# Four of the eight head tiles of the shared keys as seven Strassen block products

## The chip, the cores and the metric

The kernel runs on 1 core of one Trainium2 chip. The metric is the device time in microseconds (us). Before the change, three runs took 1932.31, 1932.89 and 1933.20 us; the median is 1932.89 us. A separate profiled execution took 1931.65 us.

## The reference

One inference step of a two-layer decoder (D_MODEL 1024, 8 heads of 128, 512 prompt rows and 32 sample rows, all float32). Layer 0 has a feed-forward block, a gated token mixer, a second feed-forward block and a gated embedding. From its result one shared set of keys, values and log-forget values is computed, and layer 1 attends to them. The change lies in the keys of that shared projection:

```python
def shared_kv(h, kv_norm, w_kvf, b_f, k_norm):
    bsz, L, _ = h.shape
    xs = rmsnorm(h, kv_norm)
    kvf = xs @ w_kvf
    k = rmsnorm(kvf[..., :D_ATT].reshape(bsz, L, N_HEADS, HEAD_DIM), k_norm)
    v = kvf[..., D_ATT:2 * D_ATT].reshape(bsz, L, N_HEADS, HEAD_DIM)
    logf = jax.nn.log_sigmoid((kvf[..., 2 * D_ATT:] + b_f).astype(jnp.float32))
    return k, v, logf
```

`k`, `v` and `logf` are outputs, and the attention of layer 1 reads them back.

## The kernel before

**Layout.** Activations lie transposed: 8 chunks of 128 features by T = 544 columns (512 prompt, 32 sample). A matmul has a 128x128 stationary weight block and streams 272 columns (HT), half of the 544. Float32 precision comes from pairs: each operand is split into a rounded high part and a remainder, `hi` and `lo`, and a product is three matmuls, hi·hi, hi·lo and lo·hi (`mm`, L286, L290, L292). A head tile of the keys (`k_tile`) is one output of 128 features: 8 weight blocks, 3 products, 2 halves, so 48 matmuls of 272 columns, accumulated in one `ps` tile (two PSUM banks; three such tiles exist). A group of values (`v_group`, L892 to L894) is 96 matmuls of 256 columns in one `ps` tile, and then 16 small ones for the sample rows (L903).

**The weight stream.** All weights pass through one list, `pieces`, in the order of use. `_load` (L209) brings 512 KB by a DMA on SP's queue; `_split` makes `hi` by a CAST on ACT (L242) and `lo` by a subtraction on DVE (L243). `unit()` hands out the next piece and prepares those ahead (2 pieces split, 2 sums, 4 loads ahead). The feed-forward blocks already use Strassen's scheme: `seven` forms, from four quarter blocks of a weight, seven pieces, four of which are sums on DVE (`_sum`, L228); `forms` makes the matching sums of the activations (L352 on ACT, L356, L358, L359 on DVE, and two splits, L330 on ACT with L331 on DVE).

**The stage of the keys and values.** `kv` follows a table, `KV_ORDER`. Each entry between the bars is a step: `k0` is a head tile, `c` the columns step, `v0:` a value group with what stands beside it; after the tile's step come the norms (`s` statistics, `r` fetch a row, `n` norm) and the preparations for the next feed-forward block (`p`, `f`). The statistics of four heads (`stats`, L795 on PE, then `rsqrt_steps`: L386 on ACT, L389, L392, L393 on DVE) go out to memory as `rows` and come back broadcast over 128 partitions (L811), and the norm of a head (L954 on DVE) multiplies by such a row. The very first tiles give the row statistic `rstd` of the residual stream (`tile_rstd`: L403 on ACT, L404 on DVE, L408 on PE, then L386 to L393 again). The columns step (L855, L865) needs it, and every tile's eviction (L845) multiplies by it. The chain of log-forget values (`forget`) runs beside the tiles: L976 on PE, small steps L978 to L994 on DVE, one exponential on ACT (L980, with an ACT table load), then L1001 on PE.

**What sets the order.** Each engine works through its instructions in order and waits at semaphores. In this stage a scheduler sets that order when the program is built; SP's queue holds all the DMAs of the stage.

Of the kernel before, what the change touches and what calls it, by code (L numbers as in the profile page):

```python
# [26 lines left out]
ALU = mybir.AluOpType  # L27
AX = mybir.AxisListType

P = 128  # L30
D = 1024
# [5 lines left out]
T = SEQ + NS  # L37
HT = T // 2
# [14 lines left out]
NKP = NC_ // 2  # L53
# [3 lines left out]
SEVEN = "1562734"  # L57
# [9 lines left out]


KV_ORDER = """
:k0|:k1|c|:k2|:k3|v0:,s0,,r0 r1|:k4 n0 r2|:k5 n1 r3|:k6 n2|:k7 n3|v1:,s1,p0,r4 r5 p1|v2:n4 p2,r6,n5 p3 f0,r7 p4|v3:n6 p5 f1,n7,p6,p7  # L70
""".strip().split("|")


# [1 line left out]
G_KV, G_GV, G_K, G_Q = 64, 72, 80, 81  # L75
# [13 lines left out]
def woven(x):  # L89

    return x.rearrange("p (a b) -> p b a", a=2)


def turns(out):

    return out.rearrange("p (b a) -> p b a", a=2)


def unwoven(out):

    return out.rearrange("p (b a) -> p a b", a=2)


def halves(x):

    return x.rearrange("p (a b) -> p a b", a=2)
# [32 lines left out]
class Builder:  # L139
# [127 lines left out]
    def unit(self):  # L267

        self.prepare()
        return self.take()  # L270
# [76 lines left out]
    def forms(self, h, gcol, n, xs):  # L347

        nc = self.nc
        x = self.big()  # L350
        for a in range(2):
            nc.scalar.activation(x[:, a, :], h[2 * n + a], AF.Copy, scale=self.gain(gcol + 2 * n + a))  # L352
        t13, t24 = self.tmp(), self.tmp()
        two = lambda t: t.rearrange("p (a b) -> p a b", a=2)
        f13, f24 = self.big(F32R), self.big(F32R)
        nc.vector.tensor_tensor(two(t13), x[:, :, HT:], two(x[:, 0, :]), ALU.subtract)  # L356
        self.split_pair(f13, t13)
        nc.vector.tensor_tensor(t24[:, :HT], x[:, 1, HT:], t13[:, :HT], ALU.subtract)  # L358
        nc.vector.tensor_tensor(t24[:, HT:], x[:, 1, :HT], t24[:, :HT], ALU.subtract)  # L359
        self.split_pair(f24, t24)  # L360
        half = lambda t, b: tuple(x[:, b * HT:(b + 1) * HT] for x in t)
        f13, f24 = ((t[:, 0, :], t[:, 1, :]) for t in (f13, f24))
        return {"1": half(xs[2 * n], 0), "2": half(xs[2 * n + 1], 0), "3": half(xs[2 * n + 1], 1),
                "5": half(f13, 0), "7": half(f13, 1), "6": half(f24, 0), "4": half(f24, 1)}
    def ssq(self, acc, h, cols=slice(0, T), first=False):

        nc = self.nc
        sq = acc[:, cols] if first else self.tmp()[:, cols]
        nc.scalar.activation(sq, h[:, cols], AF.Square)  # L369
        if not first:  # L370
            nc.gpsimd.tensor_tensor(acc[:, cols], acc[:, cols], sq, ALU.add)  # L371
# [444 lines left out]
    def kv(self, h, box, ffn_gain):  # L816

        nc, o = self.nc, self.o
        xs = self.pairs(box)
        rstd, acc = None, box["acc"]  # L820
        kraw = []
# [6 lines left out]
        sqs, bcs, rows = [], [], {}  # L828
# [6 lines left out]
        def k_tile(hh):  # L835
            nonlocal rstd
            if rstd is None:
                p, rstd = self.tile_rstd(xs, acc)
            else:
                p = self.tile_mm(xs)  # L840
            if hh % 2 == 0:
                box["k"] = self.big()

            def take(p=p, kc=box["k"][:, hh % 2, :]):
                box["last"] = nc.vector.tensor_tensor(halves(kc), whole(p), halves(rstd), ALU.mult)  # L845
                kraw.append(kc)
                sqs.append(self.square(kc))
            self.evac(take)

        def forget():  # L850
            part, t = self.ps(), self.tmp()
# [60 lines left out]
                nc.sync.dma_start(out=self.vd[2 * g + a], in_=pair[:, :, :SEQ].bitcast(F32))  # L912

        def stats(a):
            bcs.extend(self.head_rows(sqs[4 * a:4 * a + 4]))

        def row(hh):
            rows[hh] = bcs[hh]()
# [8 lines left out]
        def forms(_):  # L927
            nxt["f"].append(self.forms(h, ffn_gain, len(nxt["f"]), self.pairs(nxt)))

        do = dict(k=k_tile, s=stats, r=row, n=norm, p=prep, f=forms)  # L930
# [11 lines left out]
        for a in range(2):  # L942
            t = self.pb()
# [427 lines left out]
    def build(self):  # L1371
        nc, i, o = self.nc, self.i, self.o
        self.set_stream()

        def plain(aps):
            for ap in aps:
                self.add_plain(ap)
# [10 lines left out]
        self.ffn_pieces(1)  # L1388
        ple_units(0)
        plain([i["wk"][c] for c in range(4)] + [i["wv"][c] for c in range(2)])  # L1390
        plain([i["wk"][c] for c in range(4, 8)] + [i["wv"][c] for c in range(2, 8)])
        self.ffn_pieces(2)
        plain(i["wq"][c] for c in range(NC_))
        plain([i["woh"][k, c] for k in range(2) for c in range(NC_ // 2)] + [i["wo"][c] for c in range(NC_)])
# [10 lines left out]
        t = self.pb()  # L1405
# [5 lines left out]
        h = [self.hp[c // 2][:, c % 2, :] for c in range(NC_)]  # L1411
# [15 lines left out]
        box = {"x": {}, "f": [], "acc": self.st()}  # L1427
# [49 lines left out]
def _stationary(w):  # L1477

    k, m = w.shape
    return np.ascontiguousarray(  # L1480
        w.reshape(k // P, P, m // P, P).transpose(2, 1, 0, 3).reshape(m // P, P, k // P * P))


def _blocks(w):

    k, m = w.shape
    return w.reshape(k // 256, 2, P, m // 256, 2, P).transpose(3, 4, 1, 2, 0, 5).reshape(m // 256, 4, P, k // 256, P)


def _constants():  # L1490
# [24 lines left out]
    c[:, C_SUM:C_SUM + NS] = r[:, None] % NS == np.arange(NS)[None, :]  # L1515
    c[:NS, C_TRI4:C_TRI4 + NS] = (s[:, None] // 4 == s[None, :] // 4) & (s[:, None] <= s[None, :])
    d[P - NS:, C_TRI4S:C_TRI4S + NS] = c[:NS, C_TRI4:C_TRI4 + NS]
    return c, d


def _arrays(x_prompt, x_sample, p_prompt, p_sample, cache_k, cache_v, cache_logf, page_table, ffn1_norm, ffn1_w1,
# [3 lines left out]
    a = {}  # L1525
# [19 lines left out]
    a["wk"] = _stationary(w_kvf[:, :D])  # L1545

    a["wv"] = w_kvf[:, D:2 * D].reshape(2, 4, P, 4, 256).transpose(3, 0, 2, 1, 4).reshape(8, P, 1024)

# [49 lines left out]
```

## Time and profile before

| | |
|---|---|
| runs | 1932.31, 1932.89, 1933.20 us |
| profiled execution | 1931.65 us, of which span 1929.9 us |
| granted TensorE clock | 1.00 |
| PE busy | 1905.2 us, 99% of the span, 16508 instructions |
| DVE busy | 1478.6 us, 77%, 1863 instructions |
| ACT busy | 949.0 us, 49%, 1428 instructions |
| DMA | 237.61 MB, mean 123 GB/s |

The span is from the first to the last instruction; the profiled execution's own time stands 1.75 us above it. Busy times are sums over an engine's instructions. A busy PE is not PE at its peak, since matmuls overlap; the distance between two starts tells what one costs. A wait belongs to the engine that stood still, with the instruction that ended it named behind the arrow.

### The profile page before, as it was taken

How to read it: one execution, taken by the hardware profiler on the slowest of the kernel's cores; microseconds unless marked ns; L12 is line 12 of the kernel's file. 1: busy time of each engine (PE TensorE's matmuls, PEld its weight loads, DVE VectorE, ACT ScalarE, POOL GpSimd, SP SyncE). 2: the span in 40 equal slices, each digit the busy share in tenths (PEclk: the TensorE clock that was granted, in tenths of full speed). 3: DMA queues.
4: the chain of work that ended last, by engine and by line, in shares of the span. 5: the costliest groups of instructions: out<-in, count | busy, mean ns of one | idle time of the engine just before them, and what ended most of it. 6: DMA issues, size and time to landing. Idle time of an engine off the chain costs nothing.

```text
span 1929.9 us, 38975 instructions
## 1 busy us (share of the span) xinstructions
PE 1905.2 (99%) x16508; PEld 1869.9 (97%) x16508; DVE 1478.6 (77%) x1863; ACT 949.0 (49%) x1428; POOL 143.4 (7%) x190
## 2 busy tenths in 40 slices
PE   9999999999999999999999999999999999999999
PEld 8999999999999999999999999999977899999999
DVE  7878888556788888866578888887476888788874
ACT  7545444424555344454466444444374754444561
POOL 0000000400100000023000000002131300000020
PEclk9999999999999999999999999999999999999999
DMA  5233234312223232531484332323769332323431
GB/s 196 78 120 110 89 120 157 97 48 88 88 99 119 79 111 89 162 112 39 150 306 141 121 110 99 121 83 126 229 211 328 101 110 78 121 94 105 133 109 47
DMA packets 95743, 237.61 MB, mean 123 GB/s; under 512 B 11874, under 2 KB 29570, under 8 KB 95570
## 3 DMA queue, kind: packets, MB, share of 16 engines
q1 hardware_dynamic: 95426, 235.08, 36.6%
q8 instruction: 130, 2.13, 0.4%
q14 instruction: 43, 0.35, 0.1%
q10 hardware_dynamic: 144, 0.04, 0.0%
HBM read 218.65 MB, written 16.44 MB: 122 GB/s over the span
## 4 chain that ended last, share of the span: by engine, by line
PE 88%; DVE 6%; ACT 3%; issue 2%; DMA 1%; SPq 1%; POOL 0%; DVEq 0%; ACTq 0%; POOLq 0%
PE ps L539 31%; PE ps L286 15%; PE ps L292 15%; PE ps L290 15%; PE pb L539 5%; DVE big L243 2%; ACT big L242 1%; DVE big L228 1%; PE ps L892 1%; PE ps L893 1%; PE ps L894 1%; DVE big L331 1%; DVE big L497 0%; DMA tmp<-rows 0%; PE ps L1286 0%
## 5 line engine op out<-in xcount | busy, mean ns | idle before, releaser
L539 PE MATMUL ps<-big,big 128*128 128x272 f32 x5616 | 674.1, 279 | 5.9 <-DVE big L556 3.5
L539 PEld LDWEIGHTS ps<-big,big 128*128 128x128 f32 x5616 | 660.8, 189 | 7.0 <-issue 4.0
L243 DVE TENSOR_TENSOR big<-big,big 128x1024 fp32r<-128x1024 f32 (+2 forms) x537 | 587.1, 1096 | 91.0 <-ACT big L242 89.3
L242 ACT CAST big<-big 128x1024 fp32r<-128x1024 f32 (+2 forms) x537 | 484.2, 928 | 270.2 <-DVE big L228 267.7
L286 PE MATMUL ps<-big,big 128*128 128x272 f32 x2668 | 530.2, 280 | 2.9 <-ACT big L242 2.5
L292 PE MATMUL ps<-big,big 128*128 128x272 f32 x2668 | 528.3, 279 | 2.5 <-DVE big L243 2.3
L290 PE MATMUL ps<-big,big 128*128 128x272 f32 x2668 | 527.3, 279 | 0.3 <-DVE big L343 0.3
L286 PEld LDWEIGHTS ps<-big,big 128*128 128x128 f32 x2668 | 407.1, 189 | 7.8 <-ACT big L242 4.4
L292 PEld LDWEIGHTS ps<-big,big 128*128 128x128 f32 x2668 | 406.9, 189 | 4.5 <-DVE big L243 4.1
L290 PEld LDWEIGHTS ps<-big,big 128*128 128x128 f32 x2668 | 406.9, 189 | 0.7 <-DVE big L343 0.7
L371 POOL TENSOR_TENSOR st<-st,tmp 128x544 f32<-128x544 f32 (+1 forms) x63 | 87.4, 1387 | 1477.0 <-ACT tmp L369 1476.7
L228 DVE TENSOR_TENSOR big<-big,big 128x1024 f32<-128x1024 f32 x156 | 190.1, 1219 | 0.0
L578 DVE SCALAR_TENSOR_TENSOR big<-ps,big 128x544 f32<-128x544 f32 x160 | 115.3, 721 | 75.8 <-PE ps L292 75.8
L500 ACT ACTIVATE big<-big 128x544 f32<-128x544 f32 x88 | 57.9, 659 | 145.8 <-DVE big L497 144.6
L497 DVE TENSOR_TENSOR big<-big,st 128x1088 f32<-128x1088 f32 x88 | 113.6, 1293 | 3.9 <-ACT big L561 2.0
L547 ACT COPY tmp<-ps 128x544 f32<-128x544 f32 x117 | 71.5, 611 | 89.7 <-PE ps L539 89.7
L539 PE MATMUL pb<-big,big 128*128 128x272 f32 x936 | 114.8, 279 | 0.0
L539 PEld LDWEIGHTS pb<-big,big 128*128 128x128 f32 x936 | 111.3, 189 | 0.0
L342 ACT ACTIVATE big<-big,gains 128x544 fp32r<-128x544 f32 (+1 forms) x80 | 55.5, 702 | 91.3 <-DVE big L578 55.2
L331 DVE TENSOR_TENSOR big<-big,big 128x544 fp32r<-128x544 f32 (+1 forms) x112 | 79.2, 713 | 21.7 <-ACT big L330 21.5
L343 DVE SCALAR_TENSOR_TENSOR big<-big,gains,big 128x544 fp32r<-128x544 f32 (+1 forms) x80 | 64.6, 816 | 24.2 <-ACT big L342 24.2
L330 ACT CAST big<-big 128x544 fp32r<-128x544 f32 (+1 forms) x112 | 71.2, 643 | 18.9 <-DVE big L503 14.9
(218 smaller groups left out, 1388.5 us busy)
## 6 DMA issues: line engine op xcount, KB each, us to landing
big<-in_w SPq DMA_DIRECT2D x156, 512.0 KB
big<-in_w2a SPq DMA_DIRECT2D x64, 512.0 KB
big<-in_w2b SPq DMA_DIRECT2D x32, 384.0 KB
big<-in_w13p SPq DMA_DIRECT2D x16, 512.0 KB
big<-in_win SPq DMA_DIRECT2D x16, 512.0 KB
big<-in_wg SPq DMA_DIRECT2D x16, 512.0 KB
big<-in_ck SPq DMA_DIRECT2D x16, 512.0 KB
big<-in_cv SPq DMA_DIRECT2D x16, 512.0 KB
```

Source lines behind the costliest of these rows:

```text
L228: self.nc.vector.tensor_tensor(t, a, b, ALU.add if op == "+" else ALU.subtract)
L242: self.nc.scalar.copy(hi, src)
L243: self.nc.vector.tensor_tensor(lo, src, hi.bitcast(F32), ALU.subtract)
L286: i = nc.tensor.matmul(o, wh, xh[:, b], start=s, stop=False)
L290: nc.tensor.matmul(o, wh, xl[:, b], start=False, stop=False)
L292: nc.tensor.matmul(o, wl, xh[:, b], start=False, stop=e)
L331: self.nc.vector.tensor_tensor(pair[:, 1, cols], src, pair[:, 0, cols].bitcast(F32), ALU.subtract)
L371: nc.gpsimd.tensor_tensor(acc[:, cols], acc[:, cols], sq, ALU.add)
L497: tt(g, g, rstd.unsqueeze(1).broadcast_to([P, 2, T]), ALU.mult)
L539: nc.tensor.matmul(turns(dst[w]), a[:, c], woven(b), start=k in "152" and kp == 0 and n == 0, stop=kp == NKP - 1 and n == 2, skip_group_ch ...
L547: nc.scalar.copy(t["r" + k], t["C" if k == "5" else "A"])
L578: nc.vector.scalar_tensor_tensor(halves(h[c]), whole(out), 0.5, halves(h[c]), ALU.mult, ALU.add)
```

## The change

Head tiles 4 to 7 are no longer four plain tiles. Their weight, 1024 by 512, is cut into two by two blocks (over the input features and over the pair of tiles), and the product is made from seven block products, `u1` to `u7`, instead of eight. A step `u` is 24 matmuls (4 block pairs, 3 products, 2 tiles) of 272 columns; the seven are 168, the four tiles were 4 × 48 = 192. They accumulate in two `ps` tiles, A (products 1, 6, 7, 4) and C (5, 3), and for product 2 in a pair of one-bank tiles, B (`pb`). Copies on ACT (three, L390) and additions on DVE (L394, L396, L398) put the parts together; the multiplication by `rstd` comes after that (L890, on two heads at once). The weights of the four tiles (`wk7`) are laid out in pairs and go through `seven`, so there are seven pieces and four sums in place of four pieces. Four more `forms` (`g0` to `g3`) stand beside `k0` to `k3`. The value groups, the first four head tiles and the rest of the program keep their code. (The functions behind the new lines stand some 40 to 49 lines lower: L403, L404, L386, L389, L393 are L443, L444, L426, L429, L433; L954 is L1003, L903 is L952, L1001 is L1050, L865 is L914.)

```diff
-:k0|:k1|c|:k2|:k3|v0:,s0,,r0 r1|:k4 n0 r2|:k5 n1 r3|:k6 n2|:k7 n3|v1:,s1,p0,r4 r5 p1|v2:n4 p2,r6,n5 p3 f0,r7 p4|v3:n6 p5 f1,n7,p6,p7
+:k0 g0|:k1 g1|c|:k2 g2|:k3 g3|v0:,s0,,r0 r1|:u1|:u5 n0 r2|:u6 n1|:u2 r3|:u7 n2|:u3|:u4 n3|v1:,s1,p0,r4 r5 p1|v2:n4 p2,r6,n5 p3 f0,r7 p4|v3:n6 p5 f1,n7,p6,p7
...
+    def strassen(self, xf, done):
...
+        def step(k):
+            hi, lo = self.unit()
+            self.advance()
+            if k == "2":
+                t["B"] = [self.pb()[:, :HT] for _ in range(2)]
+            elif k in "15":
+                t["A" if k == "1" else "C"] = self.ps()[:, :, :HT]
+            out = t["A" if k in "1674" else "C" if k in "53" else "B"]
+            for kp in range(NKP):
+                xh, xl = xf[kp][k]
+                for n, (a, b) in enumerate(((hi, xh), (hi, xl), (lo, xh))):
+                    for w in range(2):
+                        c = slice(512 * w + P * kp, 512 * w + P * kp + P)
+                        nc.tensor.matmul(turns(out[w] if k == "2" else out[:, w]), a[:, c], woven(b),
+                                         start=k in "152" and kp == 0 and n == 0, stop=kp == NKP - 1 and n == 2,
+                                         skip_group_check=True)
+            if k in "156":
+                t["r" + k] = self.tmp().rearrange("p (w b) -> p w b", w=2)
+                nc.scalar.copy(t["r" + k], out)
+            elif k == "2":
+                t["g"] = self.big(), self.big()
+                for w in range(2):
+                    tt(halves(t["g"][0][:, w, :HT]), unwoven(out[w]), unwoven(t["r1"][:, w]), ALU.add)
+            elif k == "7":
+                tt(h4(t["g"][1][:, :, HT:]), u4(out), u4(t["r5"]), ALU.add)
+            elif k == "3":
+                tt(h4(t["g"][0][:, :, HT:]), u4(out), u4(t["r6"]), ALU.add)
+                done(0, t["g"][0])
+            else:
+                nc.scalar.copy(h4(t["g"][1][:, :, :HT]), u4(out))
+                done(1, t["g"][1])
...
+        def k_done(a, g):
+            box["last"] = nc.vector.tensor_tensor(g, g, rstd.unsqueeze(1).broadcast_to([P, 2, T]), ALU.mult)
...
-        plain([i["wk"][c] for c in range(4, 8)] + [i["wv"][c] for c in range(2, 8)])
+        d = self.seven([i["wk7"][x] for x in range(4)])
+        self.pieces.extend(d[k] for k in SEVEN)
+        plain(i["wv"][c] for c in range(2, 8))
```

The scheduler's order outside this stage is the same but for one swap of two small DVE steps in attention. Inside the stage three places matter.

**ACT at the row statistic of the residual stream.** `st_10946` is `rstd`. Before:

```order
L242 CAST big_10867<-big_10616 128x1024
L242 CAST big_10957<-big_10715 128x1024
L403 CAST tmp_10936<-st_10311 128x544
L386 ACT_TABLE_LOAD
L386 ACTIVATE st_10946<-pb_10940,eps 128x272
L386 ACTIVATE st_10946<-pb_10941,eps 128x272
```

With the change (L443 and L426 are L403 and L386 of before):

```order
L242 CAST big_10867<-big_10616 128x1024
L352 ACTIVATE big_10957<-big_92,gains 128x544 x2
L443 CAST tmp_10936<-st_10311 128x544
L330 CAST big_10962<-tmp_10960 128x544
L330 CAST big_10963<-tmp_10961 128x544
L242 CAST big_10971<-big_10715 128x1024
L426 ACT_TABLE_LOAD
L426 ACTIVATE st_10946<-pb_10940,eps 128x272
L426 ACTIVATE st_10946<-pb_10941,eps 128x272
```

The whole of `g0` (two L352, two L330) and one weight CAST now stand ahead of the table load and the two reciprocal roots.

**PE behind the first value group.** Before, the sample rows of that group (L903) are followed by the forget chain's L1001 and by head tile 4:

```order
L903 MATMUL pb_11340<-big_10871,xraw 32x256 x4
L903 MATMUL pb_11340<-big_10961,xraw 32x256 x4
L1001 MATMUL ps_11367<-big_11118,tmp_11120 32x512 x4
L1001 MATMUL ps_11367<-big_11118,tmp_11120 32x384 x4
L1001 MATMUL ps_11367<-big_11118,tmp_11120 32x256 x4
L1001 MATMUL ps_11367<-big_11118,tmp_11120 32x128 x4
L1004 MATMUL ps_11367<-big_11118,tmp_11120 32x32 x4
L286 MATMUL ps_11394<-big_10310,big_11174 128x272 x2
```

With the change the same place begins so (`pb_11615` and `pb_11616` are B, `big_11479` and `big_11480` are hi and lo of the block a12):

```order
L943 MATMUL ps_11244<-big_11154,big_10846 128x256
L952 MATMUL pb_11398<-big_10871,xraw 32x256 x4
L952 MATMUL pb_11398<-big_10975,xraw 32x256 x4
L385 MATMUL pb_11615<-big_10408,big_11479 128x272
L385 MATMUL pb_11616<-big_10408,big_11479 128x272
```

Two more that read `big_11479` follow, then the first two that read `big_11480`, and so on over the four block pairs. The end of that run is (`ps_11452` is A, `big_11232` and `big_11233` are hi and lo of the block a11):

```order
L385 MATMUL pb_11616<-big_10846,big_11479 128x272
L1050 MATMUL ps_11425<-big_11162,tmp_11164 32x512 x4
L1050 MATMUL ps_11425<-big_11162,tmp_11164 32x384 x4
L1050 MATMUL ps_11425<-big_11162,tmp_11164 32x256 x4
L1050 MATMUL ps_11425<-big_11162,tmp_11164 32x128 x4
L1053 MATMUL ps_11425<-big_11162,tmp_11164 32x32 x4
L385 MATMUL ps_11452<-big_10310,big_11232 128x272 x4
```

So 22 of the 24 matmuls of `u2`, the fourth Strassen step of the table, stand first, ahead of L1050 and of `u1`; its last two come after `u6`.

**DVE at the same place.** Before:

```order
L393 SCALAR_TENSOR_TENSOR st_11255<-tmp_11256,st_11255 128x544
L331 TENSOR_TENSOR big_11351<-big_11187,big_11351 128x512
L331 TENSOR_TENSOR big_11356<-big_11187,big_11356 128x512
L243 TENSOR_TENSOR big_11362<-big_11178,big_11361 128x1024
L1010 TENSOR_TENSOR tmp_11389<-ps_11367,tmp_11388 128x512
```

With the change:

```order
L433 SCALAR_TENSOR_TENSOR st_11313<-tmp_11314,st_11313 128x544
L1038 SCALAR_TENSOR_TENSOR tmp_11164<-tmp_11164 128x40 x5
L228 TENSOR_TENSOR big_11419<-big_11236,big_11084 128x1024
L1038 SCALAR_TENSOR_TENSOR tmp_11164<-tmp_11164 128x40
L331 TENSOR_TENSOR big_11409<-big_11245,big_11409 128x512
L331 TENSOR_TENSOR big_11414<-big_11245,big_11414 128x512
L1039 SCALAR_TENSOR_TENSOR tmp_11164<-tmp_11164 128x40
L243 TENSOR_TENSOR big_11422<-big_11419,big_11421 128x1024
L1041 SCALAR_TENSOR_TENSOR tmp_11164<-tmp_11164 128x40
L1003 SCALAR_TENSOR_TENSOR big_10956<-big_10956,gains,tmp_11390 128x544
L243 TENSOR_TENSOR big_11480<-big_11242,big_11479 128x1024
L1043 COPY tmp_11164<-tmp_11164 128x160
```

The `lo` of a12 (`big_11480`), which `u2` reads in its fifth matmul, stands behind the splits of the value group, behind the sum and the split of piece 6, and behind the first norm (L1003), whose row `tmp_11390` comes back from memory. On ACT the CASTs of piece 6 and then of a12 stand behind the eviction and the two splits of the value group, which read its finished sum.

More of the change, by code (lines that the diff above doesn't have):

```diff
@@ L364, in forms @@
                 "5": half(f13, 0), "7": half(f13, 1), "6": half(f24, 0), "4": half(f24, 1)}
+    def strassen(self, xf, done):
+        nc, tt, t = self.nc, self.nc.vector.tensor_tensor, {}
+        u4 = lambda t: t.rearrange("p w (b a) -> p w a b", a=2)
+        h4 = lambda t: t.rearrange("p w (a b) -> p w a b", a=2)
+        def step(k):
[29 more added lines that the diff above has]
+                done(1, t["g"][1])
+        return step
     def ssq(self, acc, h, cols=slice(0, T), first=False):
@@ L820, in kv @@
         rstd, acc = None, box["acc"]
-        kraw = []
+        kraw, sqs = {}, {}
         wf = self.tmp()[:, :NC_ * NS].rearrange("p (k n) -> p k n", n=NS)
@@ L827, in kv @@
         self.vsd = self.dram.tile([NS, D], F32, name="vsd")
-        sqs, bcs, rows = [], [], {}
+        bcs, rows = [], {}
         nxt = {"x": {}, "f": []}
@@ L845, in take, with k_forms @@
                 box["last"] = nc.vector.tensor_tensor(halves(kc), whole(p), halves(rstd), ALU.mult)
-                kraw.append(kc)
-                sqs.append(self.square(kc))
+                kraw[hh], sqs[hh] = kc, self.square(kc)
             self.evac(take)
+        def k_done(a, g):
+            box["last"] = nc.vector.tensor_tensor(g, g, rstd.unsqueeze(1).broadcast_to([P, 2, T]), ALU.mult)
+            for w in range(2):
+                kraw[4 + 2 * w + a], sqs[4 + 2 * w + a] = g[:, w], self.square(g[:, w])
+        kf = []
+        unit = self.strassen(kf, k_done)
+        def k_forms(n):
+            kf.append(self.forms(h, G_KV, n, xs))
         def forget():
@@ L914, in stats @@
         def stats(a):
-            bcs.extend(self.head_rows(sqs[4 * a:4 * a + 4]))
+            bcs.extend(self.head_rows([sqs[k] for k in range(4 * a, 4 * a + 4)]))
         def row(hh):
@@ L928, in forms @@
             nxt["f"].append(self.forms(h, ffn_gain, len(nxt["f"]), self.pairs(nxt)))
-        do = dict(k=k_tile, s=stats, r=row, n=norm, p=prep, f=forms)
+        do = dict(k=k_tile, s=stats, r=row, n=norm, p=prep, f=forms, g=k_forms, u=lambda k: unit(str(k)))
         parse = lambda s: [[lambda x=x: do[x[0]](int(x[1])) for x in y.split()] for y in s.split(",")]
@@ L1487, in _blocks, with _pairs @@
     return w.reshape(k // 256, 2, P, m // 256, 2, P).transpose(3, 4, 1, 2, 0, 5).reshape(m // 256, 4, P, k // 256, P)
+def _pairs(w):
+    h = w.shape[1] // 2
+    return np.stack([_blocks(w[:, :h]), _blocks(w[:, h:])], 3).reshape(4, P, 1024)
 def _constants():
@@ L1544, in _arrays @@
     a["win"], a["wout"] = _stationary(gmlp_w_in[0]), _stationary(gmlp_w_out[0])
-    a["wk"] = _stationary(w_kvf[:, :D])
+    a["wk"] = _stationary(w_kvf[:, :D // 2])
+    a["wk7"] = _pairs(w_kvf[:, D // 2:D])
     a["wv"] = w_kvf[:, D:2 * D].reshape(2, 4, P, 4, 256).transpose(3, 0, 2, 1, 4).reshape(8, P, 1024)
```

## The prediction

> **What bounds the kernel now.** I read the page first, then the stage by windows, then the timelines of the engines in it.
>
> ```profile
> PE 1905.2 (99%) x16508; PEld 1869.9 (97%) x16508; DVE 1478.6 (77%) x1863; ACT 949.0 (49%) x1428; POOL 143.4 (7%) x190
> ...
> PEclk9999999999999999999999999999999999999999
> ```
>
> PE is the bound: it stands idle for some 25 us of 1929.9, at full clock throughout. So a matmul less shortens the end, and a wait of PE lengthens it, one for one. The windows cut the stage into head tiles 0 to 3 with the first value group, head tiles 4 to 7, and the other value groups:
>
> ```profile
> 904.00:944.00 40.00, 39.43 (x375) 37.23 (x377) 25.17 (x43) 17.57 (x26) 8.19 (x6) 1.00 0.15 52
> 944.00:976.00 32.00, 32.00 (x326) 29.87 (x319) 19.98 (x33) 18.48 (x31) 0.84 (x4) 1.00 0.78 276
> 976.00:1009.00 33.00, 33.00 (x314) 29.51 (x312) 24.73 (x37) 21.08 (x38) 3.60 (x4) 1.00 0.90 308
> ```
>
> The columns are length, busy PE, PEld, DVE, ACT, POOL, clock, DMA share and GB/s. PE waits 0.57 us in 105. DVE is busy 69.9 us of them, ACT 57.1.
>
> **What is saved.** Seven steps of 24 matmuls replace four tiles of 48: 168 for 192, 24 fewer, all of 272 columns.
>
> ```profile
> 927.78 0.40 PE L286 MATMUL ps<-big,big 128*128 128x272 f32 x2
> 928.01 0.40 PE L290 MATMUL ps<-big,big 128*128 128x272 f32 x2
> ```
>
> Two matmuls start every 0.23 us (928.01 - 927.78), 0.116 each; 24 × 0.116 = **2.8 us**. This is certain from the order, and below it the change cannot go.
>
> **What is added off PE.** Prices from the next feed-forward block's form, and a sum:
>
> ```profile
> L228 DVE TENSOR_TENSOR big<-big,big 128x1024 f32<-128x1024 f32 x156 | 190.1, 1219 | 0.0
> ```
> ```profile
> 990.16 1.39 ACT L352 ACTIVATE big<-big,gains 128x544 f32<-128x544 f32 x2
> ...
> 994.21 0.65 ACT L330 CAST big<-tmp 128x544 fp32r<-128x544 f32 x1 [2.66 <-DVE tmp L356]
> ```
> ```profile
> 993.46 0.71 DVE L356 TENSOR_TENSOR tmp<-big 128x544 f32<-128x544 f32 x1
> ...
> 994.68 0.44 DVE L359 TENSOR_TENSOR tmp<-big,tmp 128x272 f32<-128x272 f32 x1
> 995.04 1.52 DVE L331 TENSOR_TENSOR big<-tmp,big 128x544 fp32r<-128x544 f32 x2
> ```
>
> A form costs DVE 0.71 + 2 × 0.44 + 1.52 = 3.1 us and ACT 1.39 + 2 × 0.65 = 2.7. DVE gets four forms (12.4), four sums (4 × 1.22 = 4.9), three more splits at about the same 1.22 (3.7) and some 2 us in evictions: 23 us into the 35 idle ones. ACT gets four forms (10.8), three CASTs of about 1 us and four copies: some 16 into 48. In total both fit beside PE. What costs is where they stand in the queues.
>
> **First place: the row statistic waits behind g0.** Order on ACT: CAST, g0's two L352, L403, g0's two L330, CAST, table load, roots.
>
> ```profile
> 908.64 1.98 ACT L242 CAST big<-big 128x1024 fp32r<-128x1024 f32 x2
> ...
> 914.78 0.86 ACT L386 ACTIVATE st<-pb,eps 128x272 f32<-128x272 f32 x2 [1.87 <-PE pb L408]
> ...
> 935.29 1.28 ACT L386 ACT_TABLE_LOAD   x1
> ```
> ```profile
> 909.71 3.87 DVE L243 TENSOR_TENSOR big<-big,big 128x1024 fp32r<-128x1024 f32 x2 [0.31 <-ACT big L242]
> ...
> 915.68 0.73 DVE L389 SCALAR_TENSOR_TENSOR tmp<-st 128x544 f32<-128x544 f32 x1 [1.47 <-ACT st L386]
> ...
> 917.34 0.73 DVE L393 SCALAR_TENSOR_TENSOR st<-tmp,st 128x544 f32<-128x544 f32 x1
> ```
> ```profile
> 918.21 1.02 PE pb L865 x8
> ```
>
> DVE's first L243 ends at 909.71 + 3.87/2 = 911.65. L404 (as L356, 0.71) brings 912.4, g0 to its L359 takes 994.68 + 0.44 - 993.46 = 1.66, so 914.0; the second L330 on ACT ends at 914.7, the CAST (half of 1.98) at 915.7, the table load (1.28) at 916.9, the roots (0.86) at 917.8. L389 to L393 take 918.07 - 915.68 = 2.4: 920.2 for 918.07 before. The columns step on PE, which already waits 0.57 us for it, starts 2.2 later; if the table load hid behind the CAST, 0.9. I take **1.8** (0.9 to 2.3), near the in-order chain. Everything behind moves with it.
>
> **Second place: u2 stands ahead of what is ready.** T is the end of the first value group's 96 matmuls, 943.81 before.
>
> ```profile
> 932.17 1.02 PE pb L976 x10
> 937.20 1.05 PE pb L795 x16
> ...
> 943.81 1.00 PE pb L903 x16
> 944.81 2.15 PE ps L1001 x32
> ```
> ```profile
> 937.91 0.89 ACT L386 ACTIVATE st<-pb,eps 128x272 f32<-128x272 f32 x2 [1.34 <-PE pb L795]
> 943.90 1.57 ACT L898 ACTIVATE big<-ps,sm 128x256 f32<-128x256 f32 x4 [5.10 <-PE ps L894]
> ...
> 946.73 1.08 ACT L242 CAST big<-big 128x1024 fp32r<-128x1024 f32 x1
> ```
> ```profile
> 936.64 1.37 DVE L989 SCALAR_TENSOR_TENSOR tmp<-tmp 128x40 f32<-128x40 f32 x6
> ...
> 946.37 1.29 DVE L331 TENSOR_TENSOR big<-big,big 128x512 fp32r<-128x512 f32 x2 [5.09 <-ACT big L330]
> 947.84 1.22 DVE L243 TENSOR_TENSOR big<-big,big 128x1024 fp32r<-128x1024 f32 x1 [0.17 <-ACT big L242]
> ...
> 985.25 0.79 DVE L954 SCALAR_TENSOR_TENSOR big<-big,gains,tmp 128x544 f32<-128x544 f32 x1 [4.75 <-DMA tmp<-rows]
> ```
>
> Before, PE goes from L903 straight on to L1001. Now it is free at T + 1.0 and next in its queue are u2's matmuls, which need a12's hi (ACT) and lo (DVE). u1, whose operands come far earlier in both queues, is behind them.
>
> Key statistics: L976 now stands 60 of 96 matmuls into the group, with L795 behind it. The 48 matmuls from 938.25 to 943.81 take 0.116 each, so L976 starts 36 × 0.116 + 1.02 + 1.05 = 6.3 before T. From its start to the end of the second table load were 935.29 + 1.28 - 932.17 = 4.4 us (the exponential's table is loaded in between): T - 1.9. Roots 0.89, L389 to L393 2.4: T + 1.4.
>
> hi: five small steps (5/6 of 1.37) bring DVE to T + 2.6, the sum for piece 6 (1.22) to T + 3.8; ACT casts piece 6, then a12, 1 us each: T + 5.9. ACT's own work ahead would allow T + 4.9 (946.73 + 2 - 943.81).
>
> lo: DVE goes on from T + 3.8 with L331 twice (1.29) and small steps, the split of piece 6 (1.22) to T + 6.7, a small step, the norm L1003 (0.79; its row lands 4.75 behind T + 1.4, so in time) to T + 7.7, the split of a12 to T + 8.9.
>
> PE idles from T + 1.0 to T + 5.9, does four matmuls (0.5), idles to T + 8.9: 4.9 + 2.5 = 7.4. I take **7.2**. With only ACT's own work ahead, hi comes at T + 4.9 and lo behind it (two splits and a norm behind 947.84) at T + 7.5: 3.9 + 2.1 = 6.0, the low end. A late row gives 8.0, the high end.
>
> [...] No run here shows such a gap yet; the longest wait of PE in this profile is 2.1 us:
>
> ```profile
> PE ps L539 <- DVE big L556: 3.5, 3, 2.1
> PE ps L1170 <- ACT tmp L1186: 2.6, 4, 1.3
> ```
>
> [...]
>
> **Smaller terms.** The lo parts of products 7 and 3 stand on DVE behind the forget chain's steps, norms and two sums (1.22), while PE needs a step's 24 × 0.116 = 2.8 us per product: sum, split, norm and one half-split are 1.22 + 1.22 + 0.79 + 0.65 = 3.9, 1.1 more than a step, once at 3 or 7 and less at 4. I take **0.9** (0 to 1.6). The value weights are now issued on SP behind the forget terms' and two heads' stores, in a DMA stretch that is 78% busy before; the next group may wait: **0.3** (0 to 1.0). The four key loads keep size and number, so 0. Later norms and forms run beside value groups as before, with 8 idle us on DVE: 0. B's pair of banks is free before the next statistics: 0.
>
> **Sum.** -2.8 + 1.8 + 7.2 + 0.9 + 0.3 = **+7.4 us**. The profiled execution's 1931.65 (1929.9 span and 1.75 around it) becomes 1939.05; it stands 1.24 under the median, so 1932.89 + 7.4 = **1940.3**.
>
> **Rivals.**
> [...]
> - The time is given back (the other side): later waits of PE that hang on a DMA or POOL and not on PE shrink as PE comes later. The attention is the place: PE waits there for L1186. From 3.5 us given back of the 10.2 lost (1.8 + 7.2 + 0.9 + 0.3) on, the result is within 0.2%, under +3.9; with 3.9 given back it is 1936.4. Against: ACT and DVE there themselves wait for PE.
> - The value weights come late, by a whole load more: u4 is over and PE waits some 2.5 us further: +9.9, 1942.8.
> - The change does only what it says, all cover holds: -2.8, 1930.1. That requires hi of a12 by T + 1.0, against the order.
>
> **How the numbers follow.** Forecast 0.50, half clock 0.22, given back 0.11, late weights 0.08, pure saving 0.05, others 0.04. A measurement here tells 0.2%, 3.9 us, from no change. Slower: 0.50 + 0.22 + 0.08 and half of the others, less a little of the forecast's low end: 0.82; same: 0.15; faster: 0.03. The ends of the terms give -2.8 + 0.9 + 6.0 = +4.1 and -2.8 + 2.3 + 8.0 + 1.6 + 1.0 = +10.1; taking in the given-back case partly and the half clock: 1936.2 to 1943.6.
>
> **What would show it.** Right: PE waits of about 5 and 2.5 us at L385 pb, released by L242 on ACT and L243 on DVE, behind L952; L914 starting about 2 us later; L385 matmuls 168, DVE about 1500 busy, ACT about 965. Wrong: no wait at L385 pb, or the next feed-forward block reached no later than before; a dip of the granted clock behind the gap would show the half clock.

## The result and the profile after

The changed kernel takes 1948.57 us (median of 6 runs, 1947.53 to 1949.79), the kernel before 1933.00 beside it (6 runs, 1931.12 to 1933.42). The ratio is 1.0083, 95% interval 1.0071 to 1.0096: **15.6 us slower**. Forecast were 7.4. The span of its profiled execution grows by 17.1, from 1929.9 to 1947.0 us: single executions scatter by one or two us around the median.

The first line is the page's row of busy times, the others are the same three windows as before (length, busy PE, PEld, DVE, ACT, POOL, granted clock, DMA share, GB/s):

```profile
PE 1912.0 (98%) x16484; PEld 1873.4 (96%) x16484; DVE 1498.2 (77%) x1892; ACT 964.7 (50%) x1451; POOL 144.6 (7%) x190
```
```profile
904.00:944.00 40.00, 36.56 (x317) 35.30 (x319) 30.74 (x41) 24.14 (x36) 8.18 (x6) 0.91 0.15 50
944.00:976.00 32.00, 26.40 (x242) 21.65 (x243) 19.66 (x43) 15.59 (x26) 1.96 (x3) 0.89 0.37 128
976.00:1009.00 33.00, 30.52 (x262) 27.41 (x262) 24.21 (x34) 20.12 (x32) 2.06 (x3) 1.00 0.72 251
```

There are 24 matmuls fewer, and yet PE is busy 6.8 us longer (1912.0 - 1905.2) and idle 10.3 us longer. In the stage PE waits 11.5 us (3.44, 5.60 and 2.48 in the three windows), where it waited 0.57, and two of the windows show a clock of 0.91 and 0.89. The page's clock row has 9 in all forty slices: a dip of some 7 us does not show in a slice of 49.

**First place.** PE, with the windows around it:

```profile
915.35 2.04 PE L904 MATMUL ps<-big,tmp 128*32 128x272 f32 x32
920.83 1.84 PE L914 MATMUL pb<-consts,st 128*128 128x1 f32 x8 [3.44 <-DVE st L433]
...
922.81 0.82 PE L286 MATMUL ps<-big,big 128*128 128x272 f32 x2
```
```profile
917.00:921.00 4.00, 0.56 (x9) 0.20 (x2) 2.87 (x6) 2.52 (x5) 0.00 (x0) 0.91 0.00 0
921.00:927.00 6.00, 6.00 (x34) 5.97 (x35) 5.67 (x9) 4.71 (x8) 0.00 (x0) 0.50 0.13 11
927.00:930.00 3.00, 3.00 (x28) 3.00 (x27) 0.05 (x1) 0.08 (x1) 0.00 (x0) 0.98 0.86 321
```

The columns step starts 2.62 us later than before (920.83 - 918.21). Behind the wait the clock is 0.50: the eight small matmuls of L914 take 1.84 us and took 1.02, the pairs of head tile 2 follow each other at twice 0.23 us. How long that lasts follows from the clock column. At half speed a window loses half its length, so the time at half speed is twice the sum of length × (1 - clock): 2 × (4 × 0.09 + 6 × 0.50 + 3 × 0.02) = 6.84 us.

**Second place.** PE, the windows, and what it waits for on ACT and DVE:

```profile
949.53 1.07 PE L952 MATMUL pb<-big,xraw 128*32 128x256 f32 x16
954.53 1.27 PE L385 MATMUL pb<-big,big 128*128 128x272 f32 x4 [3.93 <-ACT big L242]
957.21 4.31 PE L385 MATMUL pb<-big,big 128*128 128x272 f32 x18 [1.40 <-DVE big L243]
```
```profile
954.00:957.00 3.00, 1.27 (x4) 0.95 (x4) 2.67 (x4) 0.48 (x1) 0.92 (x1) 0.57 0.83 313
957.00:961.00 4.00, 3.79 (x17) 3.79 (x18) 1.01 (x3) 0.00 (x0) 0.43 (x2) 0.50 0.99 376
961.00:964.00 3.00, 3.00 (x44) 1.67 (x44) 0.00 (x0) 0.06 (x1) 0.00 (x0) 0.96 0.04 11
```
```profile
952.46 2.02 ACT L242 CAST big<-big 128x1024 fp32r<-128x1024 f32 x2
```
```profile
955.23 0.78 DVE L1003 SCALAR_TENSOR_TENSOR big<-big,gains,tmp 128x544 f32<-128x544 f32 x1 [0.33 <-DMA tmp<-rows]
955.94 1.22 DVE L243 TENSOR_TENSOR big<-big,big 128x1024 fp32r<-128x1024 f32 x1
```

The two waits are where they were forecast, behind L952, released by a12's CAST on ACT and by its split on DVE. Behind them the clock is at 0.50 for 6.82 us by the same sum: 18 matmuls take 4.31 us.

**A third place, which was priced at 0.3.** The second value group starts 14.7 us later (985.64, before 970.93). First three rows of before, SP's issues of the group's two weights and PE's statistics; then SP after, the load in the chain that ended last, and PE:

```profile
948.62 0.86 SPq L209 DMA_DIRECT2D big<-in_wv  x1
...
957.62 0.60 SPq L209 DMA_DIRECT2D big<-in_wv  x1
```
```profile
976.38 1.12 PE L795 MATMUL pb<-tmp,ones 128*32 128x272 f32 x16
```
```profile
976.02 1.94 SPq L1008 DMA_DIRECT2D kd<-big  x2
978.06 1.38 SPq L209 DMA_DIRECT2D big<-in_wv  x2
```
```profile
978.06 6.46 DMA big<-in_wv
```
```profile
985.64 0.38 PE L941 MATMUL ps<-big,big 128*128 128x256 f32 x1 [0.45 <-ACT big L242]
986.90 0.38 PE L942 MATMUL ps<-big,big 128*128 128x256 f32 x1 [0.88 <-DVE big L243]
...
988.85 1.10 PE L835 MATMUL pb<-tmp,ones 128*32 128x272 f32 x4 [0.35 <-ACT tmp L827]
...
993.99 1.12 PE L835 MATMUL pb<-tmp,ones 128*32 128x272 f32 x12
```

Before, the group's two weights were issued 22.3 and 13.3 us ahead of the group (970.93 - 948.62 and 970.93 - 957.62). Now they go out one behind the other, the first 7.6 us ahead, behind the stores of two heads. Its load takes 6.46 us from issue to landing, and the waits of 0.45 and 0.88 hang on it. One reason can be read from the kernel's text: the look-ahead counts pieces (4), and the four pieces ahead of this weight were head tiles of 48 matmuls, 4 × 48 × 0.116 = 22.3 us; now they are steps of 24, which makes 11.1 us before the stores ahead of it on SP. And the statistics of the last four heads (L835, before L795) no longer run as one row of sixteen: in the new order four of them stand alone and take 1.10, the other twelve 1.12.

### The profile page after: what moved, and what is told of

Same layout as the page of the kernel before. It is cut to its first block, busy times and chain, and to the rows that moved or that the text cites. A ratio compares the mean times of both kernels' runs of the same rounds, so it can differ in the third digit from the quotient of the medians.

```text
span 1947.0 us, 38984 instructions
## 1 busy us (share of the span) xinstructions
PE 1912.0 (98%) x16484; PEld 1873.4 (96%) x16484; DVE 1498.2 (77%) x1892; ACT 964.7 (50%) x1451; POOL 144.6 (7%) x190
## 3 DMA queue, kind: packets, MB, share of 16 engines
q8 instruction: 130, 2.13, 0.4%
## 4 chain that ended last, share of the span: by engine, by line
PE 84%; DVE 7%; ACT 4%; DMA 3%; issue 2%; SPq 1%; POOL 0%; DVEq 0%; ACTq 0%; POOLq 0%
PE ps L579 30%; PE ps L286 14%; PE ps L292 14%; PE ps L290 14%; PE pb L579 5%; DVE big L243 2%; ACT big L242 2%; DVE big L228 1%; DMA big<-in_cv 1%; DMA tmp<-rows 1%; PE ps L941 1%; PE ps L942 1%; PE ps L943 1%; PE ps L385 1%; DVE big L331 1%
## 5 line engine op out<-in xcount | busy, mean ns | idle before, releaser
L579 PE MATMUL ps<-big,big 128*128 128x272 f32 x5616 | 674.1, 279 | 5.8 <-DVE big L596 3.4
L579 PEld LDWEIGHTS ps<-big,big 128*128 128x128 f32 x5616 | 660.8, 189 | 6.9 <-issue 3.9
L243 DVE TENSOR_TENSOR big<-big,big 128x1024 fp32r<-128x1024 f32 (+2 forms) x540 | 590.1, 1095 | 93.6 <-ACT big L242 91.8
L286 PE MATMUL ps<-big,big 128*128 128x272 f32 x2604 | 518.3, 280 | 3.4 <-ACT big L242 3.3
L292 PE MATMUL ps<-big,big 128*128 128x272 f32 x2604 | 516.7, 280 | 2.9 <-DVE big L243 2.8
L290 PE MATMUL ps<-big,big 128*128 128x272 f32 x2604 | 516.4, 280 | 0.3 <-DVE big L343 0.3
L286 PEld LDWEIGHTS ps<-big,big 128*128 128x128 f32 x2604 | 398.5, 190 | 8.0 <-ACT big L242 5.1
L292 PEld LDWEIGHTS ps<-big,big 128*128 128x128 f32 x2604 | 398.0, 190 | 5.1 <-DVE big L243 4.5
L290 PEld LDWEIGHTS ps<-big,big 128*128 128x128 f32 x2604 | 398.1, 190 | 0.7 <-DVE big L343 0.7
L228 DVE TENSOR_TENSOR big<-big,big 128x1024 f32<-128x1024 f32 x160 | 194.8, 1217 | 0.0
L330 ACT CAST big<-big 128x544 fp32r<-128x544 f32 (+1 forms) x112 | 71.0, 641 | 20.9 <-DVE big L543 14.8
```

The costliest lines, as they stand in the source:

```text
L228: self.nc.vector.tensor_tensor(t, a, b, ALU.add if op == "+" else ALU.subtract)
L243: self.nc.vector.tensor_tensor(lo, src, hi.bitcast(F32), ALU.subtract)
L286: i = nc.tensor.matmul(o, wh, xh[:, b], start=s, stop=False)
L290: nc.tensor.matmul(o, wh, xl[:, b], start=False, stop=False)
L292: nc.tensor.matmul(o, wl, xh[:, b], start=False, stop=e)
L579: nc.tensor.matmul(turns(dst[w]), a[:, c], woven(b), start=k in "152" and kp == 0 and n == 0, stop=kp == NKP - 1 and n == 2, skip_group_ch ...
```

## Experiments

The table gives medians; "against before" is the difference to the median of the kernel before as it was measured beside that kernel (1933.00 us for the change, 1931.64 for e1 to e4, 1932.29 for e5 to e8, 1931.99 for e9 to e12, 1931.66 for e13 and e14). An interval's half width is about 0.0009 to 0.0014, so differences between two rows are known to some 2 to 3 us only.

| kernel | us | against before | ratio [95%] |
|---|---|---|---|
| the change | 1948.57 | +15.6 | 1.0083 [1.0071, 1.0096] |
| e1 u1 ahead of the forget chain | 1938.31 | +6.7 | 1.0030 [1.0018, 1.0042] |
| e2 dummies in both gaps | 1943.90 | +12.3 | 1.0059 [1.0046, 1.0073] |
| e3 = e1 + loads 6 ahead | 1936.01 | +4.4 | 1.0019 [1.0010, 1.0028] |
| e4 = e3 + dummies in the first gap | 1934.23 | +2.6 | 1.0012 [1.0003, 1.0021] |
| e5 before, wait 2.09 | 1935.12 | +2.8 | 1.0016 [1.0007, 1.0026] |
| e6 before, wait 2.85 | 1935.97 | +3.7 | 1.0016 [1.0006, 1.0025] |
| e7 before, wait 3.60 | 1938.95 | +6.7 | 1.0033 [1.0022, 1.0045] |
| e8 before, wait 5.12 | 1939.32 | +7.0 | 1.0037 [1.0023, 1.0051] |
| e9 g0 early | 1943.20 | +11.2 | 1.0054 [1.0041, 1.0068] |
| **e10 = e1 + e9 + loads 6** | **1928.98** | **-3.0** | 0.9982 [0.9973, 0.9991] |
| e11 = e10, g1 early too | 1929.11 | -2.9 | 0.9983 [0.9974, 0.9992] |
| e12 = e10 with loads 4 | 1933.90 | +1.9 | 1.0007 [0.9998, 1.0016] |
| e13 before, loads 6 | 1931.22 | -0.4 | 0.9998 [0.9988, 1.0007] |
| e14 before, wait 1.32 | 1933.15 | +1.5 | 1.0007 [0.9997, 1.0016] |

### e1: what the second place costs

```diff
             hi, lo = self.unit()
-            self.advance()
             if k == "2":
...
                                          skip_group_check=True)
+            self.advance()
             if k in "156":
```

> Only the place of one call is moved: a Strassen step advances the forget chain after its matmuls, not before them, so that u1 and not u2 stands next in PE's queue behind the first value group. Theory A (a stall of PE costs its length and, past some length, also some 6 us at half clock, worth 2.9): the two waits of u2 (3.93 and 1.40) and the half clock behind them go, -8.2 against the changed kernel, 1940.4, +7.4 against the kernel before. Theory B (a stall costs only its length, the slow matmuls behind it being something else): -5.3, 1943.3. Theory C (the wait of u2 was cover for the value weights, which come at their own time on SP's queue): the wait before the second value group grows by what is saved, gain under 3, over 1945.5.

Measured: +6.7, 8.9 less than the change: theory A. PE goes from the sample rows into u1, 15 matmuls of which even run ahead of them, with no wait there and the clock at 1.00:

```profile
950.02 1.90 PE L384 MATMUL ps<-big,big 128*128 128x272 f32 x15
951.85 1.07 PE L952 MATMUL pb<-big,xraw 128*32 128x256 f32 x16
952.85 1.31 PE L384 MATMUL ps<-big,big 128*128 128x272 f32 x9
```

So the second place cost 8.9, more than half of the loss, by the place of one call in the program's text. When the forget chain's step is traced ahead of u1's matmuls, the scheduler sets u2 in front of both; why it chooses so the runs don't show.

### e2 and e4: is the slow stretch the gap's?

```diff
+            for _ in range(24):
+                self.tc.keep_in_program_order(nc.tensor.matmul(
+                    part[:, 0, HT:512], self.onesr, xs[0][0][:, :512 - HT], start=True, stop=True, skip_group_check=True))
             nc.vector.tensor_tensor(halves(t), part[:, :, :HT], halves(rstd), ALU.mult)
...
+                for _ in range(30):
+                    nc.tensor.matmul(t["B"][0][:, HT:512], self.onesr, xf[0]["1"][0][:, :512 - HT], start=True, stop=True,
+                                     skip_group_check=True)
```

> The changed kernel with 24 extra matmuls of 240 columns ahead of the columns step and 30 ahead of u2, into unused columns of PSUM; their results go nowhere. Nothing waits for less: the two gaps keep their ends, PE is only busy in them (about 2.5 and 3.1 us). Theory A (an idle gap closes the clock gate): the clock stays at 1.00 behind both, -2.9 twice, 1948.6 - 5.8 = 1942.8. Theory B (gaps cost only their length): no change, 1948.6, and the matmuls of k2 and u2 are still at half speed. If the extra matmuls run over the gaps' ends: later by up to 0.5 each.

> The third experiment's kernel with the 24 extra matmuls ahead of the columns step. Theory A: the half clock of the first place (2.9) goes as well: 1936.9 - 2.9 = 1934.0, what is left against the kernel before being the 2.6 us of the late row statistic and the late sums (1.1) against 2.8 saved. Theory B: as the third, 1936.9.

Measured for e2: +12.3, a gain of 3.3 where A expected 5.8 and B nothing. The windows behind the two gaps tell why:

```profile
921.00:924.00 3.00, 3.00 (x33) 2.97 (x33) 2.97 (x6) 1.92 (x4) 0.00 (x0) 1.00 0.03 5
...
954.00:957.00 3.00, 2.77 (x14) 2.77 (x15) 1.03 (x3) 0.00 (x0) 0.45 (x2) 0.61 1.06 402
957.00:960.00 3.00, 3.00 (x27) 1.84 (x30) 0.00 (x0) 0.00 (x0) 0.00 (x0) 0.83 0.30 114
```

At the first place the clock stays at 1.00, with the row statistic as late as ever: the slow matmuls were the gap's doing. (In the profile of e4 they are gone there too.) At the second place the dummies fill the wait for hi; the wait for lo is still 1.92 us, with four matmuls and 0.39 of idleness ahead of it, and that alone brings 2 × (3 × 0.39 + 3 × 0.17) = 3.36 us at half speed, half of the 6.82. A was right on the cause; but half of the slow stretch came back behind a wait of 1.92, so one long gap was not needed. In e4 the first gap's dummies bring 1.8 (4.4 to 2.6); A expected 2.9, which the intervals of e3 and e4 allow as well.

### e5 to e8 and e14: a wait of measured length

In the kernel before, additions on DVE that change nothing delay the row statistic by some 0.75 us each:

```diff
+        for _ in range(self.dose):
+            nc.vector.tensor_tensor(t, t, t, ALU.max)
+        self.dose = 0
         nc.vector.scalar_tensor_tensor(r, t, 1.5 * f, r, ALU.add, ALU.mult)
```

(`dose` is set at the head of `kv`; the first matmuls of head tiles 2 and 3 are held in the program's order. No run has this hold alone, so the times of e5 to e8 and e14 contain its price, if it has one; the clock windows stand without them.)

> The kernel before, with 2 idle additions of 0.7 us on DVE in the chain that makes the row statistic, so that PE waits at the columns step for about 2.0 us and not 0.57. Theory A (an idle gap of some length closes the clock gate for some 6 us, 2.9 lost besides; the shortest seen to do it 1.9 behind another gap, the longest seen not to 2.1): clock 1.00, +1.4. Theory B (length only): +1.4. [...]

> The same with 3 additions: PE waits about 2.7. Theory A: between the bounds, so either 1.00 and +2.1 or half clock and +5.0. Theory B: +2.1. [...]

> The same with 4 additions: PE waits about 3.4, as in the changed kernel. Theory A: clock 0.50 behind the wait, +2.8 + 2.9 = +5.7. Theory B: +2.8. [...]

> The same with 6 additions: PE waits about 4.8. Theory A: +4.3 + 2.9 = +7.2, the slow stretch no longer than before. Theory B: +4.3. [...]

> The kernel before with one addition of 0.7 us in the chain of the row statistic: PE waits about 1.3, below the 2.09 that closed the gate for 3.4 us. Theory A with a threshold between 0.57 and 2.09 leaves both open: clock 1.00 and +0.7, or one slow stretch of 3.4 us and +0.7 + 1.7 = +2.4. Theory B (length only, refuted by the dose runs): +0.7.

Windows of e14 (wait 1.32), e5 (2.09) and e8 (5.12), in that order, from where the clock first falls:

```profile
921.00:924.00 3.00, 3.00 (x28) 2.97 (x28) 2.62 (x4) 2.21 (x4) 0.00 (x0) 0.81 0.69 274
924.00:927.00 3.00, 3.00 (x18) 3.00 (x18) 0.00 (x0) 0.00 (x0) 0.00 (x0) 0.62 0.00 0
```
```profile
921.00:924.00 3.00, 3.00 (x17) 3.00 (x15) 1.83 (x3) 1.73 (x4) 0.00 (x0) 0.52 0.16 60
924.00:927.00 3.00, 3.00 (x25) 3.00 (x25) 0.00 (x0) 0.00 (x0) 0.00 (x0) 0.91 0.00 0
```
```profile
921.00:924.00 3.00, 0.40 (x2) 0.43 (x3) 2.86 (x5) 0.00 (x0) 0.00 (x0) 0.69 0.41 165
924.00:927.00 3.00, 3.00 (x21) 2.97 (x22) 2.61 (x4) 2.34 (x4) 0.00 (x0) 0.50 0.02 5
927.00:930.00 3.00, 3.00 (x20) 3.00 (x19) 0.00 (x0) 0.00 (x0) 0.00 (x0) 0.67 0.00 0
```

The sums give 3.42 us at half speed for e14, 3.42 for e5, and 6.84 for e8; the same sum gives 6.84 for e6 and e7. So the slow time comes in pieces of 3.42: one behind 1.32 and 2.09, two behind 2.85, 3.60 and 5.12, no more for the longest. Theory B, length only, falls with the half speed behind these waits, and in times with e7, which loses 6.7 (interval 4.3 to 8.7) where B expected 2.8. The 2.8 of e5 doesn't exclude B's 1.4 by itself, and the times of e6 (3.7) and e14 (1.5) lie between the figures of the two theories. Theory A holds as to the cause, but not with one length as its threshold: 1.32 us was enough in the profiled execution of e14. In times, e7's 6.7 is near A's 5.7; e8 loses 7.0, only 0.3 more for a gap 1.5 longer, because some 1.5 us of its slow stretch lie in the gap itself, where they cost nothing (it begins at 924 - 2 × 3 × 0.31 = 922.1, and PE resumes at 923.60).

The profiles hold one more test, outside the stage. Each of the sixteen kernels has the same wait of 2.13 or 2.14 us, which ends at about 546 us (548 in e14), in a feed-forward block (L539 in the kernel before), with full matmuls of 272 columns on both sides. It is the 2.1 that the prediction names as the longest wait of PE. The windows behind it in the kernel before, and then in e3:

```profile
546.00:548.00 2.00, 1.42 (x12) 1.45 (x13) 2.00 (x4) 1.70 (x3) 0.00 (x0) 1.00 0.00 0
548.00:550.00 2.00, 2.00 (x19) 2.00 (x19) 2.00 (x3) 0.43 (x1) 0.00 (x0) 1.00 0.00 0
```
```profile
546.00:548.00 2.00, 1.24 (x5) 1.27 (x6) 2.00 (x4) 1.69 (x3) 0.00 (x0) 0.66 0.00 0
548.00:550.00 2.00, 2.00 (x11) 2.00 (x10) 2.00 (x2) 0.61 (x1) 0.00 (x0) 0.50 0.00 0
```

In five profiles (e3, e4, e7, e8, e9) it is followed by 3.41 us at half speed, in the other eleven by none, so the length of a wait does not decide. The clock records of the traces point to what does. In the change and in e3, slow stretches of one execution begin whole multiples of 3.413 us apart: in the change at 920.27 and 954.41, 34.14 = 10 × 3.414; in e3 at 546.64 and 922.11, 375.47 = 110 × 3.413. Laid on this grid, the five cases have 2.02 to 2.14 us of the wait inside one period of 3.41, the other eleven at most 1.64, the rest lying in a neighbouring period. (For a kernel with no slow stretch behind a wait the grid is taken from the one in which its program ends.)

### e3, e9 to e13: what the other places cost, and a kernel that gains

The loads (e3, e4, e10, e11, e13), set at the head of `kv`, and the early sum (e9 to e12):

```diff
+        self.ahead = (2, 2, 6)
         self.kd = self.dram.tile([NH, P, 2, SEQ], F32, name="kd")
```
```diff
-:k0 g0|:k1 g1|c|:k2 g2|:k3 g3|v0:,s0,,r0 r1|:u1|...
+:k0|:k1 g1|c|:k2 g2|:k3 g3|v0:,s0,,r0 r1|:u1|...
...
-        on, nxt = self.next_norm(h, G_KV)
+        on, nxt = self.next_norm(h, G_KV, early={1: 0})
```

(`next_norm` makes form 0 behind chunk 1 of the gated embedding; `kv` takes the list from its box. In e11 `early={1: 0, 3: 1}` and g1 leaves the table too.)

> The first experiment's edit, and weights are loaded 6 pieces ahead in this stage and not 4, so that the value weights are issued on SP ahead of most of the stores. Theory A: against the first experiment the waits in the second value group (0.45 and 0.88 for the split weight, 0.35 behind) and what the late load costs there go, some 3.5 less: 1948.6 - 8.2 - 3.5 = 1936.9. Rival: the late weights cost nothing of their own, since DVE would keep PE waiting as long: as the first experiment, 1940.4.

> The changed kernel, with the first of the four sums of activations (g0) made in the embedding stage before, behind its second chunk, where DVE is idle 3 to 4 us in 10, and not beside head tile 0. The row statistic is then ready as in the kernel before. Theory A (stall and half clock): the wait at the columns step falls from 3.44 to about 0.6 and the half clock behind it goes: -2.6 - 2.9 = -5.5, 1943.1 where the changed kernel has 1948.6; the second place stays. Theory B (stall alone): -2.6, 1946.0. Rival: the sum makes the embedding's gates late on DVE and the gain is less.

> All three edits: g0 in the embedding stage, u1 ahead of the forget chain, loads 6 pieces ahead. Theory A: the third experiment (+4.4 against the kernel before) less 5.5: -1.1; by the terms, -2.8 saved and 0.2 to 0.4 for the late sums, -2.4. Theory B (stalls cost their length alone): +4.4 - 2.6 = +1.8. Rival (loads so early collide with the stores of keys and values later): nothing gained over the kernel before.

> As the tenth, with two of the four sums (g0, g1) in the embedding stage. Theory A: as the tenth within 0.5, since PE waits for neither sum there. Rival (DVE, 9 tenths busy behind the columns step, is what sets the first value group): up to 1 faster than the tenth.

> As the tenth, with the loads 4 pieces ahead as in the changed kernel, to price the late value weights by themselves. Theory A (they cost of their own what the first and third experiments differ by, 2.3): 2.3 over the tenth. Rival (they were late only because the stalls ahead made the stores late): as the tenth.

> The kernel before with one edit: loads 6 pieces ahead in the stage of the keys and values. Theory A (what the tenth experiment gains over the kernel before, 3.0, is the 24 saved matmuls, 2.8, and the loads matter only to the changed kernel's second value group): within 1 of the kernel before, at most the 0.57 us of its wait at the columns step. Rival (early loads help any kernel here, and Strassen adds nothing): 2 to 3 faster than before, as the tenth.

**e9**: +11.2, 4.4 less than the change; 5.5 was theory A's figure and 2.6 B's. The wait at the columns step is 0.57 again and the clock 1.00 there. In the profiled execution something turns up further on: the second value group now waits 1.61 and 0.88 for its late weight, and that pair of waits is followed by another 2 × 4 × 0.42 = 3.4 us at half speed:

```profile
984.00:988.00 4.00, 4.00 (x17) 2.33 (x16) 3.74 (x4) 2.26 (x5) 0.20 (x1) 0.58 0.09 37
```

**e10**: 3.0 faster than the kernel before and 18.6 faster than the change. Its stage, and the first value weight on SP:

```profile
904.00:944.00 40.00, 40.00 (x373) 37.69 (x373) 32.78 (x51) 25.62 (x39) 8.11 (x6) 1.00 0.08 27
944.00:976.00 32.00, 31.96 (x324) 28.32 (x324) 29.58 (x50) 22.62 (x37) 2.75 (x4) 1.00 0.84 307
```
```profile
951.39 0.91 SPq L209 DMA_DIRECT2D big<-in_wv  x1
```
```profile
973.85 1.14 PE L835 MATMUL pb<-tmp,ones 128*32 128x272 f32 x16
```

PE waits 0.04 us in these 72, the clock is 1.00, and the sixteen matmuls of the statistics stand together again. DVE is busy 62.4 us of the 72 (32.78 + 29.58): the added work does fit beside PE, but with little to spare. **e11** is the same within the noise; the rival's gain of up to 1 us isn't seen, but a difference of that size can't be excluded here.

**e12** against e10 prices the later loads: 4.9 us (1933.90 - 1928.98), where e1 against e3 had shown 2.3; the intervals are too wide to call the two different. In the profile of e12 the 4.9 has these parts: waits of 0.7 and 0.7 in the second value group, 0.8 in the steps u, 0.6 at the columns step (a wait that e10 doesn't have), and the statistics that run in two pieces (1.1). The rest, about 1, wasn't taken apart.

**e13** shows that the earlier loads alone give the kernel before 0.4, nothing that can be told from zero; the rival's 2 to 3 is at the edge of the interval (2.3) or beyond it. So e10's gain is most likely not the loads': with them in both kernels, the seven products bring 1931.22 - 1928.98 = 2.2 us directly, or 2.6 with each taken against the kernel before beside it, and 2.8 were to be saved.

## Why the prediction was wrong

Direction and places were right, the size was half. Each place undone by one edit: second place 8.9 (e1), first place 4.4 (e9, in whose profile another dip takes 1.7 back), late loads 4.9 (e12 against e10). With e10's -3.0 that is 15.2 for the 15.6 measured. The agreement is partly luck, since what a place costs depends on which others are undone: in the order e1, e3, e10 the steps are 8.9, 2.3 and 7.4. By the steps of the prediction:

- **"What is saved", 2.8: right.** e10 against e13 shows 2.2 to 2.6. Next to nothing was given back in the attention: the shift of 17.6 us at the next feed-forward block is still 17.1 at the end of the span. That rival is dead.
- **"In total both fit beside PE": right**, as e10 shows.
- **"First place", 1.8 (0.9 to 2.3): 2.62 measured.** The order was right, the prices were not: 1.8 was taken below the chain's own 2.2, and two prices in the chain were too low. The row with two L243 at 3.87 gave 1.94 for each; the first alone takes 2.30 and the L444 behind it 1.13 (0.71 was taken). Both run beside work on POOL (busy 3.00 us of the 3 from 909 to 912); others of their kind take 1.22 and 0.71. The rest of the chain was as forecast: second L330, CAST, table load, roots, then 2.4 us on DVE.
- **"Second place", 7.2: 5.33 measured** (3.93 + 1.40), under the low end of 6.0. hi came at T + 5.0 (T = 949.53), lo at T + 7.7. These are almost the values of the low end, "only ACT's own work ahead" (T + 4.9 and T + 7.5). ACT didn't wait for the sum of piece 6: DVE began it at 951.01, T + 1.5 and not T + 2.6. The second wait is shorter than the 2.1 of the low end because the four matmuls ahead of it took 1.27 us at half clock and not 0.5.
- **The clock: the step that failed.** Each of the two waits was followed by 6.8 us at half speed; of the first some 0.6 us lie in the wait itself and of the second 1.5, so PE lost 3.1 and 2.7, together 5.8. The sum has no term for it. The clock row of before shows no dip, though its longest wait is 2.1. That was one execution: the same wait has a dip behind it in five of the other fifteen profiles, and e5 shows one behind 2.09. The chance of 0.22 for a half clock, and the upper end of the range that takes it in, rest on no run: the profile of the kernel before shows no half clock behind a wait. What the runs showed in its place is half speed behind both waits, and 5.8 us.
- **"Value weights", 0.3 (0 to 1.0): too small.** In the changed kernel's profile the waits at the group come to 0.45 + 0.88 + 0.35 = 1.7; by runs, earlier loads are worth 2.3 (e1 against e3) to 4.9 (e10 against e12). That the weights now stand behind two heads' stores on SP was in the text; that the first would be issued 7.6 us and not 22.3 ahead of its use wasn't worked out, though the load takes 6.5 us from issue to landing and its split (CAST and subtraction) comes behind it. The rival "late by a whole load" (2.5) was nearer.
- **"Smaller terms", the late sums, 0.9: right.** The waits are 0.26, 0.42 and 0.38, together 1.06.
- **Not in the sum at all**: the statistics' matmuls pulled apart, 1.1 at the second value group.

Added up from the profile, -2.8 + 2.6 + 5.3 + 5.8 + 1.1 + 1.7 + 1.1 gives 14.8 of the 17.1 between the two profiled executions; the rest wasn't taken apart.

## What to carry to other kernels

Where a change makes PE wait at a new place, price the wait and then the clock behind it: here waits of 1.3 to 5.1 us were followed by 3.4 or 6.8 us at half speed, so that two places with waits of 3.4 and 5.3 us cost 5.8 more than their length. One profile in which a wait has no dip behind it does not clear waits of that length (2.1 us here: no dip in eleven profiles, 3.4 us in five). Before giving up such a change look at why the wait stands where it does: one call moved, one sum made a stage earlier where DVE was idle, and loads two pieces further ahead turned +15.6 into -3.0. For every transfer that is moved behind others in a queue, work out when it is issued and what that leaves until its use, not only whether the queue is full; a look-ahead that counts pieces shrinks in time when the pieces get smaller.

## What the runs showed of the hardware

**The slow clock comes in pieces, on a grid.** In the eleven kernels with a slow stretch behind a wait (the change, e1 to e9, e14) it lasts 3.4 or 6.8 us (at the columns step one piece behind waits of 1.32 and 2.09, two behind 2.85 to 5.12); in the change two stretches begin 10 × 3.414 us apart, in e3 110 × 3.413. The wait of 2.1 us at 546 was enough in five profiles, and so were waits of 1.32 (e14), 2.09 (e5) and 1.92 behind a broken one (e2). At 546 it was enough where 2.02 us or more of it lay in one period of the grid, and not where it was 1.64 or less. Where the wait lies on the grid differs between the profiles, so the same wait doesn't do it each time. Why 1.32 us was enough at the columns step no run shows. The mean clock alone does not tell where an execution was slow: in e14 it was under 1.00 in eight of ten executions, and in the kernel before beside it in eleven of 21, but the one profile of e14 has slow stretches at two places, at 35 us and at the columns step, and no profile shows one behind the wait of 0.57. One piece more or less is, by an estimate from these lengths, 0.0009 of the mean clock (3.42 / 2 / 1930) and 1.7 us: part of the scatter between executions.

**An idle gap can hide part of it.** In e8 the clock fell 1.5 us before the wait ended, and its gap of 5.12 cost hardly more (7.0) than e7's of 3.60 (6.7).

**Four of the statistics' matmuls alone took as long as sixteen in a row.** Four matmuls of L835 (32 rows of output each) took 1.10 us alone in the change, and sixteen in a row 1.12 (L795 in the kernel before) to 1.14 (e10).
